# One count for two partial sums: the waits ahead of the last instruction of a sum of relu

## Chip, cores and metric

One core of a Trainium2 chip. The metric is the device time of one execution in microseconds. A run lists its time and the span from the first to the last recorded instruction; the time is some 1.35 us longer than the span (161.23 against 159.877).

## The reference

```python
x: float32 [32, 512, 1024]            # 67.1 MB
reference(x) = sum(maximum(x, 0), axis=-1)   # float32 [32, 512]
```

The 32 x 512 rows are laid over 128 partitions, 128 rows each. Relu and sum can be done on ScalarE or on VectorE (for a row of 1024 columns the trace of before has 1.04 us on ScalarE and 1.22 on VectorE, and 0.19 and 0.08 for the read of the sum), so the kernel is a stream of loads (420 GB/s over the span) with two engines behind it.

## The kernel before

Seven loads of 16 rows go through three buffers. Then a tail of 8, 4, 2 and 1 rows is loaded, and the very last row comes in three pieces of 576, 256 and 192 columns, so that little work is left when the last byte arrives. ScalarE sums the first piece, VectorE the second. Both partial sums are written behind the third piece in the tensor `last`, and VectorE's last instruction sums all 194 columns of it (356 ns). The relu of a partial sum changes nothing, since it is not negative.

```python
LAST = [576, 256, 192]
...
    parts = [buf[:, tb, r, 0:n0], buf[:, tb, r, n0:n1], last[:, 0 : LAST[2]]]
    for k, (lo, hi) in enumerate([(0, n0), (n0, n1), (n1, D)]):
        sp.dma_start(out=parts[k], in_=xv[-1][:, BIG - 1, lo:hi]).then_inc(
            s_in[NBIG + len(TAIL) + k], 16)
...
    n = LAST[2]
    act.wait_ge(s_in[-3], 16)
    on_act(parts[0], last[:, n : n + 1]).then_inc(s_tact, 1)
    dve.wait_ge(s_in[-2], 16)
    on_dve(parts[1], last[:, n + 1 : n + 2]).then_inc(s_tpart, 1)
    dve.wait_ge(s_tpart, 1)
    dve.wait_ge(s_in[-1], 16)
    dve.wait_ge(s_tact, 1)
    on_dve(last[:, :], res[:, J - 1 : J]).then_inc(s_tdve, 1)

    sp.wait_ge(s_tdve, 1)
    sp.dma_start(out=ov[-1][:, :], in_=res[:, start[-1] : J]).then_inc(s_out, 16)
    sp.wait_ge(s_store, 16 * (len(REGIONS) - 1))
    sp.wait_ge(s_out, 16)
```

`on_act` and `on_dve` are helpers that do relu and sum of a tile in one call; the trace shows two instructions for each, the accumulating one and a read of the accumulator (415 and 83 ns for VectorE's 256 columns). The profile gives the helpers' lines, not those of the calls. `s_in[-1]` counts the last load.

Of the kernel before, what the change touches and what calls it, by code (L numbers as in the profile page):

```python
# [2 lines left out]

P = 128
D = 1024
BIG = 16
NTWO = 6
NB = 3
REGIONS = [112, 16]
CHUNKS = [(0, 0), (0, 16), (0, 32), (0, 48), (0, 64), (0, 80), (0, 96)]  # L10
STEPS = [4, 5, 7]
MIXED = [3, 4, 5]
TAIL = [8, 4, 2, 1]
LAST = [576, 256, 192]


def bass_relu_sum_kernel(
    nc: bass.Bass,
    x: bass.AP,
    out: bass.AP,  # L20
):







    fp32 = mybir.dt.float32
    ALU = mybir.AluOpType  # L30
    AF = mybir.ActivationFunctionType
    X = mybir.AxisListType.X

    B, S, _ = x.shape
    J = B * S // P
    NBIG = len(CHUNKS)
    assert BIG * NBIG + sum(TAIL) + 1 == J == sum(REGIONS) and sum(LAST) == D

    xr = x.rearrange("b s d -> (b s) d")
    of = out.rearrange("b s -> (b s)")  # L40
    start = [sum(REGIONS[:i]) for i in range(len(REGIONS))]
    xv = [
        xr[P * s : P * (s + n), :].rearrange("(p j) d -> p j d", p=P)
        for s, n in zip(start, REGIONS)
    ]
    ov = [of[P * s : P * (s + n)].rearrange("(p j) -> p j", p=P) for s, n in zip(start, REGIONS)]

    buf = nc.alloc_sbuf_tensor("buf", [P, NB, BIG, D], fp32)
    last = nc.alloc_sbuf_tensor("last", [P, LAST[2] + 2], fp32)
    res = nc.alloc_sbuf_tensor("res", [P, J], fp32)  # L50

    n_in = NBIG + len(TAIL) + len(LAST)
    s_in = [nc.alloc_semaphore(f"s_in{i}") for i in range(n_in)]
    s_act = nc.alloc_semaphore("s_act")
    s_dve = nc.alloc_semaphore("s_dve")
    s_fact = nc.alloc_semaphore("s_fact")
    s_fdve = nc.alloc_semaphore("s_fdve")
    s_tact = nc.alloc_semaphore("s_tact")
    s_tpart = nc.alloc_semaphore("s_tpart")
    s_tdve = nc.alloc_semaphore("s_tdve")  # L60
    s_store = nc.alloc_semaphore("s_store")
    s_out = nc.alloc_semaphore("s_out")

    sp, act, dve = nc.sync, nc.scalar, nc.vector


    tb = NBIG % NB


    code = nc.main_func.blocks[0].instructions  # L70
    arrival = next(
        i
        for i, ins in enumerate(code)
        if ins.engine == mybir.EngineType.SP and type(ins).__name__ == "InstDrain"
    )
    for c in range(NBIG + 1):
        if c >= NB:
            sp.wait_ge(s_dve, 3 * (c - NB + 1))
        if c < NBIG:
            g, j = CHUNKS[c]  # L80
            sp.dma_start(out=buf[:, c % NB, :, :], in_=xv[g][:, j : j + BIG, :]).then_inc(
                s_in[c], 16
            )
        if c == 0:
            code.insert(arrival, code.pop())
    r = 0
    tail = []
    for i, n in enumerate(TAIL):
        sp.dma_start(out=buf[:, tb, r : r + n, :], in_=xv[-1][:, r : r + n, :]).then_inc(  # L89
            s_in[NBIG + i], 16  # L90
        )
        tail.append((r, n, s_in[NBIG + i]))
        r += n
    n0, n1 = LAST[0], LAST[0] + LAST[1]
# [3 lines that stand above are left out]
            s_in[NBIG + len(TAIL) + k], 16  # L98
        )
    sp.wait_ge(s_fact, 1)  # L100
    sp.wait_ge(s_fdve, 1)
    for g in range(len(REGIONS) - 1):
        sp.dma_start(
            out=ov[g][:, :], in_=res[:, start[g] : start[g] + REGIONS[g]]
        ).then_inc(s_store, 16)


    def on_act(t, acc):
        return act.activation(t, t, AF.Relu, accum_out=acc)  # L109

    def on_dve(t, acc):
        return dve.tensor_scalar(  # L112
            out=t, in0=t, scalar1=0.0, scalar2=None, op0=ALU.max, op1=ALU.add, accum_out=acc
        )

    def row(c, i):
        return buf[:, c % NB, i, :], res[:, c * BIG + i : c * BIG + i + 1]

    for c in range(NTWO):
        b, steps = c % NB, STEPS if c < NTWO - 1 else MIXED  # L120
        act.wait_ge(s_in[c], 16)
        if steps is MIXED:
            dve.wait_ge(s_in[c], 16)
            for i in (BIG - 4, BIG - 3):
                on_dve(*row(c, i))
        r = 0
        for i, n in enumerate(steps):
            t = buf[:, b, r : r + n, :]
            act.activation(t, t, AF.Relu).then_inc(s_act, 1)  # L129
            dve.wait_ge(s_act, 3 * c + i + 1)  # L130
            dve.tensor_reduce(  # L131
                out=res[:, c * BIG + r : c * BIG + r + n], in_=t, axis=X, op=ALU.add
            ).then_inc(s_dve, 1)
            r += n
        if steps is MIXED:
            for i in (BIG - 2, BIG - 1):
                on_act(*row(c, i))


    j0 = NBIG * BIG  # L140
    for c in range(NTWO, NBIG):
        act.wait_ge(s_in[c], 16)
        dve.wait_ge(s_in[c], 16)
        for i in range(BIG):
            ins = (on_act if i % 2 else on_dve)(*row(c, i))
            if i >= BIG - 2:
                ins.then_inc(s_fact if i % 2 else s_fdve, 1)
    for r, n, s in tail:
        if n > 1:
            act.wait_ge(s, 16)  # L150
        dve.wait_ge(s, 16)
        for i in range(r, r + n):
            f = on_act if (i - r) % 2 else on_dve
            f(buf[:, tb, i, :], res[:, j0 + i : j0 + i + 1])

    n = LAST[2]
    act.wait_ge(s_in[-3], 16)
    on_act(parts[0], last[:, n : n + 1]).then_inc(s_tact, 1)
    dve.wait_ge(s_in[-2], 16)
    on_dve(parts[1], last[:, n + 1 : n + 2]).then_inc(s_tpart, 1)  # L160
    dve.wait_ge(s_tpart, 1)
    dve.wait_ge(s_in[-1], 16)
    dve.wait_ge(s_tact, 1)  # L163
    on_dve(last[:, :], res[:, J - 1 : J]).then_inc(s_tdve, 1)


# [6 lines that stand above are left out]
# [1 line left out]
_INS = ['x']  # L174
_OUTS = [((32, 512), 'float32')]


# [21 lines left out]
```

## Time and profile before

| | before |
|---|---|
| time, median of 3 runs (range) | 161.33 us (161.24 to 161.36) |
| span of the profiled run | 159.877 us |
| VectorE / ScalarE busy | 122.0 / 101.0 us |
| end of VectorE's accumulator read to its last instruction | 129 ns |
| separate wait ahead of the last instruction | 50 ns |

In the trace of before a wait stands in one of two ways. It can be a condition of an engine's instruction, called attached here: VectorE's last instruction names `s_tpart`. Or it is a record of its own, called a separate wait here, which the profile lists as EVENT_SEMAPHORE, for VectorE under "DVEq": the one at line 163 names `s_tact` and the last load and took 50 ns.

The last two rows matter for this change. In the chain of waits they are three short pieces, one of them named "DVEq", VectorE's sequencer. A number with three decimals in this document is from the trace's own records of instructions and of the raising of semaphores, which have ns; the printed views round to 10 ns. "Gap" always means the time from the end of VectorE's accumulator read of its partial sum to the start of its last instruction.

### The profile page before, as it was taken

How to read it: one execution, taken by the hardware profiler on the slowest of the kernel's cores; microseconds unless marked ns; L12 is line 12 of the kernel's file. 1: busy time of each engine (PE TensorE's matmuls, PEld its weight loads, DVE VectorE, ACT ScalarE, POOL GpSimd, SP SyncE). 2: the span in 40 equal slices, each digit the busy share in tenths (PEclk: the TensorE clock that was granted, in tenths of full speed). 3: DMA queues.
4: the chain of work that ended last, by engine and by line, in shares of the span. 5: the costliest groups of instructions: out<-in, count | busy, mean ns of one | idle time of the engine just before them, and what ended most of it. 6: DMA issues, size and time to landing. Idle time of an engine off the chain costs nothing.

```text
span 159.9 us, 148 instructions
## 1 busy us (share of the span) xinstructions
DVE 122.0 (76%) x58; ACT 101.0 (63%) x55; POOL 0.2 (0%) x4
## 2 busy tenths in 40 slices
DVE  0000006989879897998969989699899999598995
ACT  3000059990699808996099941999339980496972
POOL 0000000000000000000000000000000000000000
DMA  7996996996996997989979969969969969899993
GB/s 262 525 525 262 525 525 262 525 525 262 525 492 295 525 459 328 525 377 410 525 312 476 525 262 525 525 262 525 525 262 525 525 262 525 385 402 394 414 407 116
DMA packets 2305, 67.18 MB, mean 420 GB/s; under 512 B 512, under 2 KB 768, under 8 KB 1024
## 3 DMA queue, kind: packets, MB, share of 16 engines
q1 hardware_dynamic: 2304, 67.18, 97.9%
q14 instruction: 1, 0.01, 0.0%
HBM read 67.11 MB, written 0.07 MB: 420 GB/s over the span
## 4 chain that ended last, share of the span: by engine, by line
DMA 69%; ACT 18%; DVE 11%; SPq 1%; issue 0%; DVEq 0%
DMA buf<-in_x_dram 69%; ACT buf L129 18%; DVE res L131 10%; DVE buf L112 1%; SPq L89 1%; DVE last L112 0%; DVEq L163 0%
## 5 line engine op out<-in xcount | busy, mean ns | idle before, releaser
L131 DVE TENSOR_REDUCE res<-buf 128x4 f32<-128x4096 f32 (+3 forms) x18 | 100.4, 5604 | 33.6 <-ACT buf L129 33.6
L129 ACT ACTIVATE buf<-buf 128x4096 f32<-128x4096 f32 (+3 forms) x18 | 80.8, 4553 | 46.3 <-DMA buf<-in_x_dram 46.3
L109 ACT ACTIVATE buf<-buf 128x1024 f32<-128x1024 f32 (+1 forms) x18 | 18.4, 1024 | 9.8 <-DMA buf<-in_x_dram 9.8
L112 DVE TENSOR_SCALAR_CACHE_REDUCE buf<-buf 128x1024 f32<-128x1024 f32 (+1 forms) x19 | 21.3, 1173 | 2.7 <-DMA buf<-in_x_dram 2.5
L109 ACT ACTIVATION_READ_ACCUMULATOR buf<-buf 128x1 f32 x18 | 3.4, 186 | 0.0
L129 ACT ACT_TABLE_LOAD x1 | 1.3, 1283 | 0.8 <-PEq L184 0.8
L112 DVE DVE_READ_ACCUMULATOR buf<-buf 128x1 f32 x19 | 1.6, 83 | 0.0
L112 DVE TENSOR_SCALAR_CACHE_REDUCE last<-last 128x194 f32<-128x194 f32 x1 | 0.4, 356 | 0.1
L184 POOL MEMSET const-bfloat16-1.0<- 128x1 bf16 x1 | 0.1, 102 | 0.0
L184 POOL MEMSET const-uint8-127<- 128x1 uint8 x1 | 0.1, 102 | 0.0
L184 POOL MEMSET const-float32-0.0<- 128x1 f32 x1 | 0.1, 100 | 0.2 <-issue 0.2
L184 POOL MEMSET const-float32-1.0<- 128x1 f32 x1 | 0.1, 99 | 0.0
L112 DVE DVE_READ_ACCUMULATOR last<-last 128x1 f32 x1 | 0.1, 83 | 0.0
## 6 DMA issues: line engine op xcount, KB each, us to landing
buf<-in_x_dram SPq DMA_DIRECT2D x1, 4096.0 KB, 26.7
buf<-in_x_dram SPq DMA_DIRECT2D x1, 2048.0 KB, 31.2
buf<-in_x_dram SPq DMA_DIRECT2D x1, 1024.0 KB, 33.2
buf<-in_x_dram SPq DMA_DIRECT2D x1, 512.0 KB, 34.0
buf<-in_x_dram SPq DMA_DIRECT2D x1, 288.0 KB, 34.3
buf<-in_x_dram SPq DMA_DIRECT2D x1, 128.0 KB, 34.1
buf<-in_x_dram SPq DMA_DIRECT2D x7, 36.3
last<-in_x_dram SPq DMA_DIRECT2D x1, 96.0 KB, 33.9
```

The lines of the kernel that those rows point to most:

```text
L89: sp.dma_start(out=buf[:, tb, r : r + n, :], in_=xv[-1][:, r : r + n, :]).then_inc(s_in[NBIG + i], 16)
L109: return act.activation(t, t, AF.Relu, accum_out=acc)
L112: return dve.tensor_scalar(out=t, in0=t, scalar1=0.0, scalar2=None, op0=ALU.max, op1=ALU.add, accum_out=acc)
L129: act.activation(t, t, AF.Relu).then_inc(s_act, 1)
L131: dve.tensor_reduce(out=res[:, c * BIG + r : c * BIG + r + n], in_=t, axis=X, op=ALU.add).then_inc(s_dve, 1)
L184: nc = _bacc.Bacc("TRN2", target_bir_lowering=False, num_devices=1)
```

## The change

The intent: both partial sums raise one semaphore, and VectorE's last instruction waits until it is 2. The wait for the last load stays, written behind that one. Three conditions become two.

```diff
-    s_tact = nc.alloc_semaphore("s_tact")
-    s_tpart = nc.alloc_semaphore("s_tpart")
+    s_part = nc.alloc_semaphore("s_part")
...
-    on_act(parts[0], last[:, n : n + 1]).then_inc(s_tact, 1)
+    on_act(parts[0], last[:, n : n + 1]).then_inc(s_part, 1)
     dve.wait_ge(s_in[-2], 16)
-    on_dve(parts[1], last[:, n + 1 : n + 2]).then_inc(s_tpart, 1)
-    dve.wait_ge(s_tpart, 1)
+    on_dve(parts[1], last[:, n + 1 : n + 2]).then_inc(s_part, 1)
+    dve.wait_ge(s_part, 2)
     dve.wait_ge(s_in[-1], 16)
-    dve.wait_ge(s_tact, 1)
     on_dve(last[:, :], res[:, J - 1 : J]).then_inc(s_tdve, 1)
```

## The prediction

> **What bounds the kernel now.** I read four views of the kernel before, from coarse to fine. First the page: busy shares and the chain that ended last.
>
> ```profile
> span 159.9 us, 148 instructions
> DVE 122.0 (76%) x58; ACT 101.0 (63%) x55; POOL 0.2 (0%) x4
> DMA packets 2305, 67.18 MB, mean 420 GB/s; under 512 B 512, under 2 KB 768, under 8 KB 1024
> ...
> DMA 69%; ACT 18%; DVE 11%; SPq 1%; issue 0%; DVEq 0%
> DMA buf<-in_x_dram 69%; ACT buf L129 18%; DVE res L131 10%; DVE buf L112 1%; SPq L89 1%; DVE last L112 0%; DVEq L163 0%
> ```
>
> The kernel streams 67 MB at 420 GB/s. No compute engine is full (VectorE 76%, ScalarE 63%), and 69% of the chain is loads. The last entry is the one that matters here: "DVEq L163", a wait that VectorE's sequencer runs by itself, is on the chain, with a share that rounds to 0%. Line 163 is the third of the three waits ahead of VectorE's last instruction, the wait on `s_tact`.
>
> Next the chain in order of time, at its end (columns: start us, length us, what).
>
> ```profile
> 122.28 34.02 DMA buf<-in_x_dram
> 156.30 0.02 issue
> 156.32 1.57 DVE buf L112 x4
> 157.89 0.01 issue
> 157.90 0.05 DVEq L163
> 157.95 0.07 issue
> 158.02 0.36 DVE last L112 x2
> ```
>
> The load of the one full row of the tail that VectorE does alone lands at 156.30. VectorE reduces that row and the 256-wide part of the last row without a pause (1.57 us, to 157.89), then stands for 0.13 us (0.01 + 0.05 + 0.07), then does the last instruction, which adds the two partial sums to the last 192 columns. Compare the two kinds of start: after a landing, "issue" is 0.02; after the sequencer's own wait it is 0.07, on top of the 0.05 of that wait.
>
> Third, the timeline of the last two microseconds, for what runs beside it.
>
> ```profile
> 157.47 0.41 DVE L112 TENSOR_SCALAR_CACHE_REDUCE buf<-buf 128x256 f32<-128x256 f32 x1
> 157.67 0.19 ACT L109 ACTIVATION_READ_ACCUMULATOR buf<-buf 128x1 f32 x1
> 157.81 0.08 DVE L112 DVE_READ_ACCUMULATOR buf<-buf 128x1 f32 x1
> 158.02 0.36 DVE L112 TENSOR_SCALAR_CACHE_REDUCE last<-last 128x194 f32<-128x194 f32 x1
> 158.30 0.08 DVE L112 DVE_READ_ACCUMULATOR last<-last 128x1 f32 x1
> 158.41 0.34 SPq L168 DMA_DIRECT2D out_dram<-res  x1
> ```
>
> ScalarE's part ends at 157.86 and VectorE's at 157.89, nearly together, so both partial sums are due at the same moment, and the last store is issued 0.03 us after the last accumulator read (158.38). Nothing lies beside the 0.13 us gap: what is cut from it is cut from the end of the kernel.
>
> Fourth, the view of the issued loads and their landings:
>
> ```profile
> last<-in_x_dram SPq DMA_DIRECT2D x1, 96.0 KB, 33.9
> ```
>
> It is issued at 123.78 (timeline), so the last load lands at about 157.68, 0.21 us before VectorE has finished its part. The load is not what VectorE waits for at the end.
>
> The trace also keeps the times at which semaphores were raised, in ns; the printed views round them. ScalarE's accumulator read ends at 157.860 and `s_tact` is raised at 157.868; VectorE's ends at 157.888 and `s_tpart` is raised at 157.900; the last load's semaphore is full at 157.680. The separate wait at line 163 runs from 157.896 to 157.946 and the last instruction starts at 158.017.
>
> **How the three waits lie in the program.** The built program of the kernel before has one separate wait instruction here. It carries two conditions, `s_tact` and the last load. The wait written first, on `s_tpart`, is attached to the last instruction. Single waits elsewhere are all attached to the instruction behind them and leave no record of their own on VectorE. So the separate wait cannot retire before 157.868, when ScalarE's sum is there.
>
> [...] line 163 is one EVENT_SEMAPHORE of 50 ns, the only one on VectorE outside the opening barrier.
>
> [...] from `s_tact` to the start of the last instruction there are 28 + 50 + 71 = 149 ns, while an attached wait took 24 ns from landing to start (147.620 to 147.644, 152.521 to 152.545, 156.298 to 156.321, the last one 23).
>
> [...]
>
> [...] In the opening barrier VectorE's sequencer woke at 0.721 for a semaphore raised at 0.693, 28 ns. At the end it woke 157.896 - 157.868 = 28 ns after `s_tact`. The wait thus started as if ScalarE alone had set it, not the end of VectorE's own work.
>
> **The change, part by part.**
> It removes a semaphore and one condition; no data, shape, instruction on the engines or transfer changes. Some 157.89 us of the trace before this point are untouched.
>
> 1. The order of the waits turns round in effect. By the rule seen in before (the first written wait is attached, the rest go into the separate instruction), the wait on `s_part` for 2 is attached, and the separate instruction holds only the last load. There is still one separate wait, so the instruction count of VectorE should not fall.
> 2. The separate wait moves off the path. The load is full at 157.680; with 28 + 50 + 71 ns the last instruction stands ready [...] at 157.829. The partial sums are both counted at 157.900. Slack: 71 ns.
> 3. The attached wait then sets the start: `s_part` reaches 2 with VectorE's increment at 157.900, plus 24 ns: 157.924 instead of 158.017. Saved: 93 ns.
> 4. The two increments lie 32 ns apart (157.868 and 157.900), one from each engine, as before; counting them on one semaphore I put at 0.
> 5. The last instruction, its accumulator read, the store's issue and its landing move up unchanged by 0.09 us.
>
> Sum: 0.093 us of 161.33, which is 0.06%. An upper limit is the gap of 158.017 - 157.888 = 0.129 us; the 12 ns of VectorE's increment and the 24 ns of an attached start remain, and they make up the difference. The floor of 2% would be 3.2 us, twenty-five times the whole gap.
>
> **The rivals.**
> First: a separate wait does not run while VectorE is busy. Then it would start after 157.888 even with the load long landed, take its 50 + 71 ns, and the last instruction would start at about 158.017 as now. Gain 0, time 161.33. For it: 157.896 is also only 8 ns after VectorE's end, so before alone can't exclude it. Against it: the 28 ns that match the barrier. I give it about one in five.
>
> Second: the last load takes the place of ScalarE's sum. If it lands more than 71 ns later than in this trace, relative to VectorE's end, the separate wait ends later than 157.900 less 71, and it, not the partial sums, sets the start. Loads of the tail land 0.76, 0.36 and 0.26 us apart (156.298, 157.060, 157.424, 157.680), so a shift of 0.07 us in some executions is possible. This would give back part of the 93 ns, and could cost nothing beyond before, which waits for the same load.
>
> Third: the conditions are laid out the other way, `s_part` in the separate wait and the load attached. Then the path has 28 + 50 + 71 ns after 157.900, that is 158.049 instead of 158.017: 32 ns slower. Against it: in before, the first written of three is the attached one.
>
> Fourth: two engines raising one semaphore hinder each other. Nothing in this trace shows a cost near 0.1 us for that; one extra raising delay of the size seen (8 to 12 ns) would leave about 80 ns of gain.
>
> **Range and chances.** Four fifths of 93 ns, plus nothing for the rest, is 0.07 us; I predict 161.25 us. The three runs of before spread over 161.24 to 161.36, 0.12 us, more than the gain. The loads before the tail can differ by more from one session to the next, so I take 161.02 to 161.45 as the range that should hold it 8 times in 10; its centre lies close to the prediction. No path leads to 2%: within 2% at 0.99, and 0.005 each for faster and slower, for some slow execution that has nothing to do with the change.
>
> **What would show each step right or wrong.** In the chain of the changed kernel, the sequencer's wait should be gone between VectorE's row work and the last instruction, with about 0.04 us of "issue" in place of 0.13. The remaining separate wait should carry the line of the last load's wait and start about 28 ns after that load lands, while VectorE's 256-wide part is still running (first rival wrong), or else after VectorE's end (first rival right). The last instruction should start 24 ns after VectorE's increment and 36 ns after its accumulator read. The span should shrink from 159.88 to about 159.79 if the last loads land as before; because landings can shift, the gap is the better measure than the span. Wrong would be: a gap that is still 0.13 us; a start that follows the separate wait; or a time outside the range with the gap shortened, which would mean that the loads, not the waits, moved.

The count full at 157.900 and 24 ns of an attached start make 157.924, against 158.017, so 93 ns, and four fifths of it, 0.07 us, came off 161.33. That a separate wait can run while VectorE computes, on which step 2 rests, was the estimate; the trace of before has only the two equal distances of 28 ns for it. VectorE's wait for its own partial sum stays.

## The result

| | before | changed |
|---|---|---|
| time, median of 6 runs (range) | 161.32 us (161.20 to 161.36) | 161.21 us (161.12 to 161.35) |
| span of the profiled run | 159.877 us | 159.775 us |
| gap | 129 ns | 35 ns |
| separate wait on VectorE | 50 ns, after ScalarE's sum | 21 ns, after the last load |

The ratio is 0.9995, with a 95% interval of 0.9983 to 1.0008. A ratio here is the mean time of one kernel's fast runs over that of the other's of the same rounds, so it is not quite the ratio of the medians. By the times alone the two kernels are the same. The traces differ clearly, in one place. First the page of the changed kernel, span and chain:

```profile
span 159.8 us, 148 instructions
...
DMA 69%; ACT 18%; DVE 11%; SPq 1%; issue 0%
DMA buf<-in_x_dram 69%; ACT buf L128 18%; DVE res L130 10%; DVE buf L111 1%; SPq L88 1%; DVE last L111 0%
```

The instruction count is still 148, so no instruction went away. "DVEq" has left the chain. The end of the chain in order of time (start us, length us, what):

```profile
156.26 0.02 issue
156.28 1.38 DVE buf L111 x3
157.67 0.10 issue
157.77 0.10 DVE buf L111
157.86 0.02 issue
157.89 0.36 DVE last L111 x2
```

The "issue" of 0.10 at 157.67 is not an idle engine: the chain looks only at what began last, and the accumulating instruction of 157.43 is still running there, as the timeline shows. What counts is the 0.02 at 157.86, where before had 0.01 + 0.05 + 0.07. The timeline of that place:

```profile
157.43 0.41 DVE L111 TENSOR_SCALAR_CACHE_REDUCE buf<-buf 128x256 f32<-128x256 f32 x1
...
157.77 0.08 DVE L111 DVE_READ_ACCUMULATOR buf<-buf 128x1 f32 x1
157.89 0.35 DVE L111 TENSOR_SCALAR_CACHE_REDUCE last<-last 128x194 f32<-128x194 f32 x1
```

And the separate wait by its source line (durations in ns as min/median/max, first and last start in us):

```profile
L161 DVEq EVENT_SEMAPHORE  x1: 21/21/21, 157.6 to 157.6; - x1
```

It now has the line of the wait for the last load and runs from 157.645 to 157.666, while VectorE computes (157.428 to 157.843). The last load was full at 157.618. The two sums were counted at 157.833 and 157.863, and the last instruction started at 157.886, 23 ns after the second.

The span became 102 ns shorter. It can be split: the load of the last full row landed 38 ns earlier (156.260 against 156.298; the two profiles of the changed kernel alone, 156.26 and 156.45, differ by more), the gap is 94 ns shorter, and the final store took 29 ns longer from its issue to the end of the span (1.498 against 1.469 us); the rest is rounding of a ns or so. So the change gained 94 ns ahead of the last instruction.

The longer store came again in other profiles. Its landing raises its semaphore 16 times, and these counts take 200 ns from the first to the last in all seven profiles in which that semaphore has the number 120 (the changed kernel's among them), but 175 ns in all three in which it has 121 (the kernel before and two variants of it). The change removes one semaphore, and so the store's number falls from 121 to 120. By the traces, then, some 25 of the 94 ns are lost again behind the last instruction, and about 69 are left. No run changed the number alone, so it is not shown that the number is the cause.

### The profile page after: what moved, and what is told of

Its sections match the earlier page's. It is cut to its first block, busy times and chain, and to the rows that moved or that the text cites. A ratio compares the mean times of both kernels' runs of the same rounds, so it can differ in the third digit from the quotient of the medians.

```text
span 159.8 us, 148 instructions
## 1 busy us (share of the span) xinstructions
DVE 122.0 (76%) x58; ACT 101.0 (63%) x55; POOL 0.2 (0%) x4
## 4 chain that ended last, share of the span: by engine, by line
DMA 69%; ACT 18%; DVE 11%; SPq 1%; issue 0%
DMA buf<-in_x_dram 69%; ACT buf L128 18%; DVE res L130 10%; DVE buf L111 1%; SPq L88 1%; DVE last L111 0%
```

## The experiments

Theory A: the time depends only on which condition sits in the separate wait instruction. A condition attached to VectorE's instruction costs some 24 ns from the raising of its semaphore to the start; a condition in the separate wait costs the way to its start, its own length and the way to the next start, 28 + 50 + 71 = 149 ns for ScalarE's sum in the kernel before. If a condition comes early, the separate wait is over before anyone needs it. The rivals: B, only the number of conditions counts, not their order. C, the shared semaphore itself saves the time. D, a separate wait costs its time even when it ends early. And the plain doubt that a difference of 0.1 us is chance.

In the built programs, the first written wait was the attached one in each of these kernels, and one or two further conditions shared one separate wait (21 ns long with one; 49 or 50 with two, and 95 in the one case below where the second came true during it). Turning the lines round therefore moves a condition from one place to the other without taking a wait away.

**Two semaphores, VectorE's own sum in the separate wait.** One run.

```diff
-    dve.wait_ge(s_tpart, 1)
+    dve.wait_ge(s_tact, 1)
     dve.wait_ge(s_in[-1], 16)
-    dve.wait_ge(s_tact, 1)
+    dve.wait_ge(s_tpart, 1)
     on_dve(last[:, :], res[:, J - 1 : J]).then_inc(s_tdve, 1)
```

> The kernel before with its three waits in the other order: the wait on ScalarE's sum is attached to the last instruction, VectorE's own sum and the last load are in the separate wait. Theory A (what counts is whether the condition that comes last sits in the separate wait): VectorE's own increment comes last, about 12 ns after its accumulator read, so the gap from that read's end to the last instruction is 12 + 28 + 50 + 71 = 161 ns, 32 ns more than the 129 ns of before. Theory B (three waits on two semaphores cost the same in any order, and only fewer conditions help): 129 ns again. Time within 0.1 us of before either way.

The end of the chain:

```profile
157.96 0.03 issue
157.99 0.05 DVEq L163
158.04 0.07 issue
158.11 0.36 DVE last L112 x2
```

VectorE's read ended at 157.948 and the last instruction started at 158.108: a gap of 160 ns, against 161 expected by A and 129 by B. Order alone, at the same three conditions, cost 31 ns. B falls. The time was 161.32 us beside 161.19 for before, one run each, which decides nothing.

**One count, the load attached.** One run.

```diff
-    dve.wait_ge(s_part, 2)
     dve.wait_ge(s_in[-1], 16)
+    dve.wait_ge(s_part, 2)
```

> The changed kernel with its two waits in the other order: the last load is attached, the count of two is in the separate wait. Theory A: the separate wait, now with one condition (21 ns in the changed kernel), is released at VectorE's increment, so the gap is 12 + 28 + 21 + 71 = 132 ns, or 120 ns if the time behind a one-condition wait is shorter. Theory C (the shared semaphore itself is what saved the time): about 35 ns as in the changed kernel. Time about that of before under A, 0.1 us less under C.

The end of the chain:

```profile
157.95 0.03 issue
157.97 0.02 DVEq L161
157.99 0.07 issue
158.06 0.36 DVE last L111 x2
```

The gap is 131 ns (157.934 to 158.065): 12 + 27 + 21 + 71, where A had worked out 132. This kernel has the shared semaphore and two conditions, like the changed one, and none of its gain. C falls for this place. The single time was 161.31 us beside 161.19.

**Two semaphores, three waits as before, ScalarE's sum early.** One run.

```diff
-LAST = [576, 256, 192]
+LAST = [448, 384, 192]
```

> The kernel before, two semaphores and three waits as they were, but 128 of ScalarE's columns go to VectorE (448, 384 and 192), so that ScalarE's sum comes some 0.25 us before VectorE's. Theory A: the separate wait ends while VectorE still computes, and the gap falls to about 35 ns with no change of any wait; VectorE's part is 128 columns or 0.13 us longer, so the last instruction starts at about 158.06, 0.04 us later than before. Theory C (the shared semaphore is needed): the gap stays at 129 ns and the last instruction starts at about 158.15.

The separate wait by its line:

```profile
L163 DVEq EVENT_SEMAPHORE  x1: 95/95/95, 157.7 to 157.7; - x1
```

And the end of the chain:

```profile
158.07 0.02 issue
158.10 0.36 DVE last L112 x2
```

No wait was changed, yet the gap is 35 ns (158.061 to 158.096): ScalarE's sum was counted at 157.654, and the separate wait was over at 157.777, while VectorE computed until 158.054. So the shared semaphore is not needed; an early condition is enough. As expected, VectorE's larger part took the gain back: from the landing of the last full row to the last instruction it was 1.758 us (156.338 to 158.096), against 1.719 before, 39 ns more. Time 161.31 us, one run. The 95 ns of this wait are taken up below.

**One count of 18 for both sums and the load, no separate wait.** Once, then five rounds, because the single time was odd.

```diff
-            s_in[NBIG + len(TAIL) + k], 16
+            s_in[NBIG + len(TAIL) + k] if k < 2 else s_part, 16
...
-    dve.wait_ge(s_part, 2)
-    dve.wait_ge(s_in[-1], 16)
+    dve.wait_ge(s_part, 18)
```

> The changed kernel with the last load counted on the same semaphore, and one wait for 18 (16 + 1 + 1), so that no separate wait is left. Theory A: the separate wait was off the path already, so the gap stays at about 35 ns (12 + 23). Theory D (a separate wait costs its 50 or 21 ns even when it ends early): the gap falls below 30 ns. Correct result, as no subset of the three can reach 18.

> The kernel with one count of 18 again, in five rounds. Its single time was 161.84 us, 0.65 us over the kernel before, while its span of 159.9 us and its gap of 35 ns gave no reason. If that was a single slow execution, the median is now like that of the changed kernel, 161.1 to 161.3 us. If a load and two engines on one semaphore cost something that the span does not show, the median is again near 161.8 us.

The page of both profiles counts 147 instructions, one fewer than the changed kernel. The end of the chain of the second:

```profile
156.32 1.58 DVE buf L111 x4
157.90 0.02 issue
157.92 0.36 DVE last L111 x2
```

The gaps are 35 ns in the first profile and 34 ns in the second, as in the changed kernel. An instruction less, and not a ns gained in the gap: the separate wait, once early, costs nothing there, and D falls. But the time went the wrong way. The first run took 161.84 us; of the six runs of the rounds five took 161.75 to 161.86 and one 161.26, median 161.81, ratio to before 1.0027 (1.0015 to 1.0039). The spans, 159.7 to 160.0 us, are as in the other kernels. In the profiled run the time less the span is 1.94 us, where the changed kernel has 1.35. The extra 0.5 us lies outside the recorded instructions, and none of it is in the gap. What it comes from stays open: this kernel differs from the changed one by one instruction on VectorE and by a load that raises the same semaphore as two engines, and no run here separates the two.

The traces do show where it lies. After the last instruction the semaphores are written once more, in groups. The group of 156 to 206 begins 0.85 us after the last instruction's end in both profiles of this kernel, and 0.29 to 0.31 us after it in the other twelve. And the page of each of those twelve has the line of a DMA queue for instructions (here the changed kernel's), while neither page of this kernel has it:

```profile
q14 instruction: 1, 0.01, 0.0%
```

In this kernel two packets of 8 KB of that kind start 1.33 and 1.63 us after the last instruction's end; in the other kernels without extra rounds one starts 0.13 to 0.22 us before it. So these transfers come at another moment here. That is a coincidence in time and not a test of the cause.

**Sixteen more handovers, three forms.** To measure the cost in the time and not only in a gap, the kernel before got 16 rounds of the same handover behind its last instruction. In each, ScalarE sums 192 columns and VectorE 32, and VectorE adds the two sums; the next round's ScalarE waits for it. The added results go nowhere, the output stays correct. Only the waits and their semaphores differ between the three kernels. Five rounds each, in one session.

```diff
+    for k in range(N):   # N = 16
+        act.wait_ge(s_r, k) if k else act.wait_ge(s_tdve, 1)
+        on_act(buf[:, 0, 1, 0:192], scr[:, 3 * k : 3 * k + 1]).then_inc(s_ract, 1)
+        on_dve(buf[:, 0, 0, 32 * k : 32 * k + 32], scr[:, 3 * k + 1 : 3 * k + 2]).then_inc(s_rpart, 1)
+        dve.wait_ge(s_rpart, k + 1)
+        dve.wait_ge(s_in[-1], 16)
+        dve.wait_ge(s_ract, k + 1)
+        on_dve(scr[:, 3 * k : 3 * k + 2], scr[:, 3 * k + 2 : 3 * k + 3]).then_inc(s_r, 1)
```

That is the form of before. The form of the change raises `s_ract` from both engines and waits for `2 * (k + 1)` of it, then for the load. The third form keeps both semaphores and exchanges the first and the third wait, so that ScalarE's sum, which comes last here, is attached.

> The kernel before, with 16 further rounds of the same handover behind its last instruction: ScalarE sums 192 columns, VectorE 32 columns, and VectorE's next instruction adds the two sums under the three waits of before. ScalarE's sum comes last in each round, and it sits in the separate wait. Worked out from the traces, a round takes about 0.79 us: 16 of them 12.6 us, total about 174 us. Theory A: from ScalarE's increment to VectorE's start 28 + 50 + 71 = 149 ns in each round.

> The same 16 rounds with the waits of the changed kernel: one count of both sums, attached; the last load in a separate wait. Theory A: 24 ns from ScalarE's increment to VectorE's start, so 125 ns less in each round and 16 x 125 = 2.0 us less than the rounds in the form of before, about 172 us. If the gain in the one handover was chance of landings, the two kernels with rounds take the same time within 0.2 us.

> The same 16 rounds with two semaphores and three waits, in the other order: ScalarE's sum, which comes last, is attached; VectorE's own sum and the load are in the separate wait and come some 0.36 us earlier. Theory A: as fast as the rounds with the shared count, within 0.2 us, about 172 us. Theory C (the shared semaphore is what saves): as slow as the rounds in the form of before, about 174 us.

Two consecutive starts of the adding instruction, from the timelines: first the form of before, then the form of the change (start us, length us; in brackets VectorE's idle time before it and what ended it):

```profile
165.91 0.15 DVE L117 TENSOR_SCALAR_CACHE_REDUCE scr<-scr 128x2 f32<-128x2 f32 x1 [0.52 <-ACT buf L114]
...
166.72 0.16 DVE L117 TENSOR_SCALAR_CACHE_REDUCE scr<-scr 128x2 f32<-128x2 f32 x1 [0.52 <-ACT buf L114]
```

```profile
165.45 0.16 DVE L117 TENSOR_SCALAR_CACHE_REDUCE scr<-scr 128x2 f32<-128x2 f32 x1 [0.42 <-ACT buf L114]
...
166.13 0.15 DVE L117 TENSOR_SCALAR_CACHE_REDUCE scr<-scr 128x2 f32<-128x2 f32 x1 [0.41 <-ACT buf L114]
```

The period is 0.81 us in the one and 0.68 in the other. Of the difference, 0.10 or 0.11 us is idle time ahead of the adding instruction, which ScalarE ends; the rest is VectorE's own sum, which ends sooner after the add's start (0.27 us against 0.29). The means over all rounds, with the turned form:

| rounds in the form of | time, median of 4 runs | period of a round, mean | ScalarE's end to VectorE's start, mean |
|---|---|---|---|
| before | 174.46 us (174.24 to 174.53) | 803 ns | 151 ns |
| the change | 172.53 us (172.46 to 172.70) | 685 ns | 33 ns |
| two semaphores, turned | 172.50 us (172.44 to 172.57) | 685 ns | 33 ns |

A round is 118 ns shorter, 16 of them 1.89 us, and the medians differ by 1.93 us; A had 2.0. The final store's semaphore has the number 124 in all three, and its 16 counts take 165 or 166 ns in each, so the store adds nothing to the difference. The small miss: from the end of the separate wait to the next start it was 64 or 65 ns in 15 of the 16 rounds, not 71. The turned form with two semaphores is as fast as the shared count. So the shared semaphore saves nothing by itself here, and it costs nothing either; theory C falls for good. The ratios to before are 1.0809, 1.0693 and 1.0690.

**The changed kernel again.** Five rounds.

> The changed kernel as it is, five more rounds beside the kernel before. Theory A: 0.09 us faster in the mean, a ratio of about 0.9994, of the order of the spread of single runs; the trace shows a gap of 35 ns again. If the first result was chance, the ratio can lie on either side of 1 and the gap can be other than 35 ns.

Median 161.20 us (161.07 to 161.32) against 161.34 (161.24 to 161.50, 9 runs), ratio 0.9988 (0.9974 to 1.0001). The gap was 34 ns. The two series of runs give mean differences of 0.07 and 0.16 us; both intervals hold the 0.07 us that the trace leaves (and 0.09 as well), and neither leaves 1 out. The times agree with the gap but could not have shown it.

**The last load made late.** Two kernels, one run each: the changed one with a further load ahead of the last, and the same with the waits turned as above.

```diff
     for k, (lo, hi) in enumerate([(0, n0), (n0, n1), (n1, D)]):
+        if k == 2:
+            sp.dma_start(out=extra[:, :], in_=xv[-1][:, 0, 0:256]).then_inc(s_store, 16)
...
-    sp.wait_ge(s_store, 16 * (len(REGIONS) - 1))
+    sp.wait_ge(s_store, 16 * len(REGIONS))
```

> The changed kernel with one further load of 128 KB (into a buffer that nothing reads) ahead of the last load, so that the last load lands some 0.3 us later, after both sums. Theory A: now the separate wait is on the path: the last instruction starts 28 + 21 + 71 = 120 ns after the last load lands, and the gain of the change is gone. If the separate wait cost nothing whatever comes last, it would start about 24 ns after the landing.

> The same late load with the two waits turned: the load attached, the count of two in the separate wait. Theory A: the last instruction starts 24 ns after the last load lands, if it lands at least 96 ns after VectorE's increment; otherwise 120 ns after that increment. So with the load last this order, which lost the gain in the earlier run, is the better one.

The end of the chain, with the waits of the change:

```profile
158.20 0.03 issue
158.22 0.02 DVEq L164
158.25 0.07 issue
158.32 0.36 DVE last L114 x2
```

And with the waits turned:

```profile
158.22 0.02 issue
158.24 0.36 DVE last L114 x2
```

With the load last, the order of the change pays 119 ns from the landing (158.198) to the start (158.317), and the turned order 23 ns (158.218 to 158.241). The order that lost the gain above is the better one here. Neither order was the better one in both cases: each time the one that attached what came last was (35 against 131 ns of gap with the sums last, 23 against 119 ns from the landing with the load last). The times, 161.56 and 161.47 us, are single runs.

**One count for the two stores.** The experiments suggested one more place: the program's last wait, on SyncE, held two conditions. Five rounds.

```diff
-        ).then_inc(s_store, 16)
+        ).then_inc(s_out, 16)
...
-    sp.wait_ge(s_store, 16 * (len(REGIONS) - 1))
-    sp.wait_ge(s_out, 16)
+    sp.wait_ge(s_out, 16 * len(REGIONS))
```

> The changed kernel with the two stores counted on one semaphore, so that the last wait of the program has one condition and not two. Theory A, with what the traces show: SyncE's two-condition wait took 28 ns and its one-condition wait 17 ns, so the end comes 11 ns earlier; the time is that of the changed kernel within the noise, and the profile alone can show it.

The last wait took 17 ns where before had 28, as expected (from the record of that instruction in each profile). But from the store's issue to the end of the span it was 1.449 us, 49 ns less than in the changed kernel and not 11: the store's semaphore has the number 119 here, and its 16 counts took 166 ns instead of 200. The median was 161.19 us (161.14 to 161.30), ratio to before 0.9995 (0.9982 to 1.0008). That is the time of the changed kernel; 49 ns can't be told from noise in it. No version here beats the changed kernel beyond the noise.

## Why the prediction was right

1. *The order of the waits turns round in effect; one separate wait remains.* Right: 148 instructions, and the wait has the line of the load.
2. *The separate wait moves off the path, with 71 ns of slack.* Right, and the slack is larger, 126 ns instead of 71. One term was mis-sized: the wait has one condition now and took 21 ns, not the 50 of two. The other 26 ns are chance of the landing and rounding: the last load was full 25 ns earlier relative to the second sum. The wait ended at 157.666; with before's 71 ns more the instruction would have been ready at 157.737 (estimate), 126 ns before the second sum was counted.
3. *The attached wait sets the start, 24 ns after the count is full.* Right: 23 ns. The gap went from 129 to 35 ns, 94 saved where 93 were worked out.
4. *Two engines on one semaphore hinder each other by 0.* Right at 30 ns apart here (9 and 12 ns from the end of the read to the count, 8 and 12 in before), and in the rounds the shared count was no slower than two semaphores (685 ns a round in both).
5. *Everything behind moves up unchanged.* Right for VectorE and the store's issue, wrong for the store's landing: its 16 counts took 200 ns instead of 175, in step with the number of its semaphore. So 69 ns net, not 93.

The first rival, a separate wait that can't run while VectorE computes, is shown wrong by the changed kernel's own trace (157.645 lies inside 157.428 to 157.843). The second, a late last load, did not happen, but it is real: made late on purpose, it took 119 ns from the landing to the start, where the turned order took 23. The third, the other layout, was put at 32 ns slower than before; run on purpose it was 2 ns slower (131 against 129), again because the one-condition wait was 29 ns shorter (21 against 50). The fourth was not seen. The step to the total took four fifths of the gain, 0.07 us, for a doubt that the trace then removed. That the net gain is 0.07 us too is luck: the store's 25 ns were not foreseen. (161.33 less 0.07 is 161.26, a slip of 0.01.) 161.25 was foretold and 161.21 came, but the runs spread over 0.23 us and the range held the time of no gain too: the gap is the evidence, not the time.

## What to carry to other kernels

In all kernels here, VectorE's instruction with several waits had one place that was cheap (22 to 25 ns from the count to the start), and the rest went into a separate wait (119 to 149 ns from the count to the start where it came last). Find out which written wait gets the cheap place (here the first), and give it to the condition that comes last. Counting several producers on one semaphore is a way to put all late ones there, as long as nothing can reach the count without all of them. It was worth about 0.1 us for each handover on the path (94 ns in the changed kernel, 118 in the rounds): nothing that the times could show in this streaming kernel with one such place, 1.1% in the chain with sixteen. And a removed semaphore renumbers those behind it: here the store's went from 121 to 120, and its 16 counts took 25 ns longer.

## What else the traces show

- The price of a separate wait on VectorE: 27 to 29 ns from the semaphore to its start, 21 ns with one condition, 49 or 50 with two that are both true, and 64 to 72 ns to the next start when that start waits for nothing else; an attached wait took 22 to 25 ns in all where its engine was idle. In the rounds this came to 118 ns each, 1.93 us in sixteen. The attached condition was the first written in all kernels here.
- The record of a separate wait with two conditions began before both were true: where ScalarE's sum was early, it began at 157.682, 28 ns after the first semaphore (157.654) and 60 ns before the load's was full (157.742), and lasted 95 ns. How the two conditions are tested was not shown.
- In the rounds in the form of the change, with the load long landed, the separate wait of the next round started 17 to 20 ns after the previous round's last instruction had started, in all 15 cases, and never while that instruction was still waiting. In these cases it ran beside a running instruction, not past a waiting one. VectorE's sum and its accumulator read lay between the two, and what held the wait back until then was not shown.
- The kernel with one count of 18 showed 0.5 us more outside the span in six of seven runs (time less span 1.93 and 1.94 us in its profiled runs against 1.34 to 1.36 in the others). Its cause is open; the traces place it after the last instruction, together with later transfers of the queue for instructions.
- How close together the counts of one DMA came went with the number of its semaphore. The least distance between two of the 16 counts, over all 14 profiles, is 13 ns for the numbers 104, 112 and 120, 11 for 105 and 121, 10 for 106, 8 for 99, 107 and 123, 6 for 100, 108 and 124, 5 for 101, 109 and 117, 3 for 102 and 110, and 2 for 103, 111 and 119: of the numbers seen, those eight or sixteen apart have the same. Why is open. For the final store the 16 counts took 200 ns in all with 120, 175 with 121, and 165 or 166 with 119 and 124.
